# x^T at another place in its tile for the second attention and the second feed-forward

## The chip, the core and the metric

The program runs on one core of a Trainium2 chip. A core has a matrix engine (PE in the profile, with its weight loads as PEld), three engines for elementwise work (DVE, ACT, POOL), a queue engine (SP) that issues the transfers here, and an on-chip memory of 128 partitions. An address below is always a byte offset inside a partition, the same in all 128. The metric is the device time of one execution in microseconds.

## The reference

A decoder trunk of two layers on 256 tokens of width 1024. Each layer is a norm, an attention, a norm and a feed-forward with 2816 hidden columns; the residual stream goes through all of them.

```python
for i in range(DEPTH):
    j = i // N_MIXERS
    if i % N_MIXERS == 0:
        h = h + dilated_mixer(rmsnorm(h, a_norm[j]), a_w_in[j], a_w_out[j])
    else:
        h = h + forgetting_mixer(rmsnorm(h, b_norm[j]), b_w_in[j], b_f[j], b_w_out[j])
    h = h + swiglu(rmsnorm(h, ffn_norm[i]), ffn_w_gu[i], ffn_w_down[i])
return rmsnorm(h, final_norm)
```

All is float32. The kernel splits each operand of a large product into a high and a low part and sums three products (high·high, high·low, low·high), which `mm3` issues one after the other.

## The kernel before

The four stages run one after the other: first attention (up to about 268 us in the profiled execution), first feed-forward (to about 452), second attention (to about 569) and second feed-forward. All weights are streamed from memory through the SP queue, split by ACT (`wh`) and DVE (`wl`), and multiplied.

Each of the four stages starts from the normalized residual stream, transposed, which is called x^T (`xt`). `norm_t` (L160) scales the rows, transposes them on PE into PSUM, and splits them into the tile `xt` with ACT and DVE. The tile has one buffer, which the four stages use in turn. In a partition it is 8 k-tiles of 2 parts (high, low) of 256 float32: 16,384 bytes, every part 1,024 bytes long. The first x^T is allocated at the start of the program. Those of the two feed-forwards come from `out_proj` (L614), which is called for `a_out` and `b_out`, and that of the second attention from the first `mid` (L758).

A matmul has a stationary operand, which a weight load brings in (128 columns of 4 bytes, that is 512 bytes of each partition), and a moving one, which is streamed (256 columns are 1,024 bytes). Three helpers use x^T:

- `proj_feat` (L221): the weights are stationary, x^T is moving, 256 columns. The query and key projections, and all hidden columns of the feed-forwards from the fourth tile on (`up`). A call with both column halves is 2 · 8 · 3 = 48 matmuls.
- `proj_tok` (L201): x^T is stationary, the weights move, 256 columns. Two value projections of the second attention, and the first three tiles of each feed-forward (the "head").
- `proj_pair` (L211): as `proj_tok`, 512 columns (the last products are cut into two of 256). The first two value projections of the second attention.

Beside these, `gates_1` (L782) streams 512 columns of x^T against the small tile `wf` (8 matmuls), and the down projection (`down`, L688) has the activations `ah` and `al` stationary and the weights moving; no x^T is in it.

Where the tiles lie. Tiles get addresses in the order of the pools and tags. The tiles in front of x^T in its pool are multiples of 512 bytes long, as are all tiles of the weight pool, so they all have the address of the weights modulo 512. Behind them stands an unused tile `gap` of 112 float32, 448 bytes; then comes x^T. Modulo 512 x^T therefore begins 64 bytes in front of the weights, and as every slice of it and every slice of the weights starts at a multiple of 512 bytes of its tile, this holds for each pair of operands of these matmuls. Behind x^T the small tiles add up to 64 bytes, and the tiles of the activations (`p`, which holds `ah` and `al`) are at the place of the weights again, at a distance of 0. So are `kr` and `qzh`, `qzl` of the first attention (tag `h`), and `wf`, whose k-tiles step by 256 bytes.

The lines of the gap and of the x^T tile:

```python
    ap.tile([P, 112], F32, tag="gap", name="gap", bufs=1)
    xt = xt_tile()
```

Of the kernel before, what the change touches and what calls it, by code (L numbers as in the profile page):

```python
# [10 lines left out]
F32 = mybir.dt.float32  # L11
F32R = mybir.dt.float32r
# [4 lines left out]
P = 128  # L17
D = 1024
S = 256
KT = D // P  # L20
# [11 lines left out]
def trunk(ctx: ExitStack, tc: tile.TileContext, T, out):  # L32
# [4 lines left out]
    ap = ctx.enter_context(tc.tile_pool(name="ap", bufs=1))  # L37
# [8 lines left out]
    def psum(tag):  # L46
        return ps.tile([P, 512], F32, tag=tag, name=f"ps_{tag}", bufs=2)
# [4 lines left out]
    def load_grow(i):  # L52
        g = ap.tile([P, D], F32, tag="grow", name="grow", bufs=1)
        src = T["norms"]
        nc.sync.dma_start(g, bass.AP(tensor=src.tensor, offset=src.offset + i * D, ap=[[0, P], [1, D]]))
        return g

    def const(name, shape):
        c = cst.tile(shape, F32, name=name)
        nc.sync.dma_start(c, T[name])  # L60
        return c
# [32 lines left out]
    def fm_tile(tag, n, bufs):  # L94
        return tuple(ap.tile([P, n, S], F32R, tag=f"{tag}{x}", name=f"{tag}{x}", bufs=bufs) for x in "hl")
# [1 line left out]
    class XT(tuple):  # L97
        pass

    def xt_tile():  # L100
        full = ap.tile([P, KT, 2, S], F32R, tag="xt", name="xt", bufs=1)
        x = XT((full[:, :, 0, :], full[:, :, 1, :]))
        x.full = full
        return x
# [24 lines left out]
    def weights(nm, i, after=None):  # L129

        upto = order.index((nm, i)) + AHEAD
        while state["next"] <= min(upto, len(order) - 1):
            key = order[state["next"]]
            cuts = []
            ready[key] = piece(key, cuts)
            for cut in cuts:
                cut(after)
            state["next"] += 1
        return ready.pop((nm, i))
# [20 lines left out]
    def norm_t(h, parts, grow, xt, t):  # L160
        with first():
            r = rstd(parts)
            xn = ap.tile([P, D], F32, tag="xn", name="xn", bufs=2)
            for half in range(2):
                c = slice(half * 512, (half + 1) * 512)
                nc.vector.scalar_tensor_tensor(xn[:, c], h[:, c], r, grow[:, c], op0=ALU.mult, op1=ALU.mult)
        for half in range(2):
            tr = psum("tr")
            for k in range(4):
                kk = half * 4 + k  # L170
                nc.tensor.transpose(tr[:, k * P:(k + 1) * P], xn[:, kk * P:(kk + 1) * P], ident)  # L171
            split(xt, lambda x: x[:, half * 4:half * 4 + 4, t * P:(t + 1) * P],
                  tr.rearrange("p (k c) -> p k c", k=4))

    def mm3(o, stat, mov, start, stop, narrow=False):

        (sh, sl), (mh, ml) = stat, mov
        nc.tensor.matmul(o, sh, mh, start=start, stop=False)  # L178
        n = o.shape[-1]
        for s, m, end in ((sh, ml, False), (sl, mh, stop)):  # L180
            for c in range(0, n, n // 2 if narrow else n):
                u = slice(c, c + (n // 2 if narrow else n))
                last = nc.tensor.matmul(o[:, u], s, m[:, u], start=False, stop=end and u.stop == n)  # L183
        return last

    def both(pair, *idx):
        return tuple(x[idx] for x in pair)
# [116 lines left out]
    for i, c in enumerate(room):  # L304
        b = 1 + (i > 1)
        n = S + 512
# [12 lines left out]
        for j in range(b):  # L319
            xk.append(both_k[:, j, :S])  # L320
            wk.append(both_k[:, j, S:])

    ap.tile([P, 112], F32, tag="gap", name="gap", bufs=1)
    xt = xt_tile()

    r_a = []
    lead = [psum("sc") for _ in range(2)]
# [73 lines left out]
    x = []  # L401

    ot = fm_tile("ot", KT, 1)
# [200 lines left out]
    def residual(acc, h, name):  # L604
        hn = hrow(name)
        parts = []
        with first():
            for n in range(2):
                s = slice(n * 512, (n + 1) * 512)
                nc.vector.tensor_tensor(hn[:, s], acc[n], h[:, s], op=ALU.add)  # L610
                parts.append(sq(hn[:, s]))
        return hn, parts

    def out_proj(nm, ot, h, grow, done, banks):  # L614

        ws = [weights(nm, i) for i in range(4)]
        xt = xt_tile()
        res = []

        def part(t, acc, nk):  # L620
            last = None
            for n, k in nk:
                c = (k % 2) * D + n * 512
                last = mm3(acc[n], both(ot, ALL, k, slice(t * P, (t + 1) * P)),
                           both(ws[k // 2], ALL, slice(c, c + 512)), k == 0, k == KT - 1)
            return last

        def cols(ks):
            return [(n, k) for n in range(2) for k in ks]

        for t in range(2):
            acc = [psum(banks[t]) for _ in range(2)]
            if t == 0:

                nk = cols(range(done))
                last = part(t, acc, nk[:done])
                nk = nk[done:]
                for i in sorted(due):
                    with tc.issue_after(last.ins):
                        for fn, a in due[i]:  # L640
                            fn(*a)
                    last = part(t, acc, nk[:2]) or last
                    nk = nk[2:]
                due.clear()
                part(t, acc, nk)
                last = part(t, acc, cols(range(done, KT)))
            else:
                part(t, acc, cols(range(2)))
                with tc.issue_after(last.ins):
                    part(t, acc, cols(range(2, 6)))  # L650
                    norm_t(*res[0], grow, xt, 0)
                    part(t, acc, cols(range(6, KT)))
            res.append(residual(acc, h[t], f"h_{nm}{t}"))
        return res, xt


    def ffn(l, hs, xt, grow, mid):
        acc = {}
        acts = {}
# [77 lines left out]
        with tc.issue_after(last.ins):  # L737
            down(NJ - 2, 1)
            if l == 0:
                down(NJ - 1, 1, (0,))  # L740
            else:
                h1 = hs[1][0][:, 512:]
                with first():
                    nc.vector.tensor_tensor(h1, acc[1][1], h1, op=ALU.add)
            mid(res[0])
            down(NJ - 1, 1, (1,) if l == 0 else None)
        res.append(residual(acc[1], hs[1][0], f"hf{l}1") if l == 0 else (acc[1], hs[1][0]))
        return res

    g_f = load_grow(1)  # L750
    hs, xt = out_proj("a_out", ot, x, g_f, 6, ("sc", "mm"))
    maskb = const("maskb", [P, 3 * P])
    sel = const("sel", [80, NH])
    bf = const("bf", [NH, 1])
    wf32 = const("b_f_in", [P, KT * NH])
    nxt = {}

    def mid(h0):  # L758
        nxt["g"] = load_grow(2)
        nxt["xt"] = xt_tile()  # L760
        norm_t(*h0, nxt["g"], nxt["xt"], 0)

    hs = ffn(0, hs, xt, g_f, mid)
    xt, g_b = nxt["xt"], nxt["g"]

# [66 lines left out]
    ot = fm_tile("ot", KT, 1)  # L832
# [62 lines left out]
    for i, (hq, w) in enumerate(b_units):  # L895
# [36 lines left out]
        for fn, a in due.pop(i, ()):  # L932
            fn(*a)
    g_f = load_grow(3)
    hs, xt = out_proj("b_out", ot, [h for h, _ in hs], g_f, 5, ("mm", "sc"))

    def finish(t, h, parts):
        r = rstd(parts)
# [10 lines left out]
    hs = ffn(1, hs, xt, g_f, mid)  # L949
# [4 lines left out]
    for o, (a, b) in zip(acc, ((0, 512), (512, 256), (768, 256))):  # L954
        s = slice(a, a + b)
# [108 lines left out]
```

## Time and profile before

| | us |
|---|---|
| median of two runs | 760.5 (760.35 to 760.64) |
| the profiled execution, its own time | 761.3 |
| its span, first to last instruction | 759.4 |
| granted clock of PE over the span | 0.997 |

The profiled execution took 0.8 us more than the median, and its span is 1.9 us less than its own time. A rate is read below from the starts of matmuls: they are pipelined, so the duration of a row (276 ns for most) is longer than the step from one start to the next, and it is the step that adds up to the time. In the timeline a row has the start in us, the time to the end of the last instruction merged into the row, engine, line, operation, written and read tiles, columns of the stationary operand, form of the moving one, and the count.

### The profile page before, as it was taken

Reading aid. Unit: us, or ns where it says so; the run is one execution under the profiler, and the core shown is the slowest. Engines: PE = TensorE matmul, PEld = TensorE weight load, DVE = VectorE, ACT = ScalarE, POOL = GpSimd, SP = SyncE. Lnnn points to the kernel's source line nnn. Section 1 sums busy time; section 2 is a strip of 40 time slices with the busy share of each in tenths; the row PEclk is TensorE's granted clock in tenths of the full one; section 3 lists DMA queues with packets and bytes.
Section 4 is the critical chain, followed back from the end, with each engine's and each line's share of the span. In section 5 each row is a group of like instructions: output and inputs, shape, how many; then the busy total and the mean of one; then the engine's idle time right before and its main releaser. Section 6 shows DMA issues by size and latency. Waiting matters only on the chain.

```text
span 759.4 us, 14132 instructions
## 1 busy us (share of the span) xinstructions
PE 749.7 (99%) x5810; PEld 695.6 (92%) x5810; DVE 511.1 (67%) x758; ACT 402.7 (53%) x664; POOL 32.4 (4%) x51
## 2 busy tenths in 40 slices
PE   8999999999999999999999999999999999999996
PEld 7999999999998799999999988999889999999995
DVE  6899987986988476555556374888756655556533
ACT  7737539448538455534445354587645434455521
POOL 1110000010010000000000003100000000000000
PEclk9999999999999999999999999999999999999998
DMA  8855553653555367556567444634426665566601
GB/s 329 281 189 192 168 184 105 211 183 104 188 187 177 95 215 243 195 193 195 186 207 239 147 164 142 220 115 142 135 76 228 224 196 193 186 203 202 216 1 55
DMA packets 38352, 135.01 MB, mean 178 GB/s; under 512 B 4368, under 2 KB 5648, under 8 KB 38288
## 3 DMA queue, kind: packets, MB, share of 16 engines
q1 hardware_dynamic: 38144, 134.01, 53.3%
q8 instruction: 45, 0.74, 0.4%
q14 instruction: 19, 0.16, 0.1%
q10 hardware_dynamic: 144, 0.10, 0.0%
HBM read 133.05 MB, written 1.05 MB: 177 GB/s over the span
## 4 chain that ended last, share of the span: by engine, by line
PE 93%; ACT 2%; issue 2%; DMA 1%; DVE 1%; SPq 0%; POOL 0%; POOLq 0%; ACTq 0%; DVEq 0%
PE ps_mm L183 32%; PE ps_mm L178 17%; PE ps_tr L183 9%; PE ps_sc L183 9%; PE ps_o L183 7%; PE ps_tr L178 5%; PE ps_sc L178 4%; PE ps_o L178 3%; PE ps_tr L275 2%; PE ps_o L286 2%; PE ps_sc L844 1%; DMA otl<-in_lead 1%; ACT wh L73 1%; PE ps_tr L171 1%; PE ps_sc L441 1%
## 5 line engine op out<-in xcount | busy, mean ns | idle before, releaser
L73 ACT ACTIVATE wh<-raw 128x1024 fp32r<-128x1024 f32 x236 | 244.0, 1056 | 220.0 <-PE ps_tr L183 67.3
L75 DVE TENSOR_TENSOR wl<-raw,wh 128x1024 fp32r<-128x1024 f32 x236 | 284.6, 1222 | 99.1 <-ACT wh L73 98.7
L178 PE MATMUL ps_mm<-xt,wh 128*128 128x256 f32 x816 | 227.2, 279 | 0.0
L183 PE MATMUL ps_mm<-xt,wl 128*128 128x256 f32 x816 | 225.8, 277 | 0.1
L183 PE MATMUL ps_mm<-xt,wh 128*128 128x256 f32 x816 | 225.7, 277 | 0.0
L178 PEld LDWEIGHTS ps_mm<-xt,wh 128*128 128x128 f32 x816 | 153.3, 188 | 0.6 <-issue 0.3
L183 PEld LDWEIGHTS ps_mm<-xt,wl 128*128 128x128 f32 x816 | 153.3, 188 | 0.5 <-DVE wl L75 0.5
L183 PEld LDWEIGHTS ps_mm<-xt,wh 128*128 128x128 f32 x816 | 153.4, 188 | 0.1
L183 PE MATMUL ps_tr<-xt,wh 128*128 128x256 f32 x304 | 83.8, 276 | 0.0
L183 PE MATMUL ps_tr<-xt,wl 128*128 128x256 f32 x304 | 83.8, 276 | 0.0
L178 PE MATMUL ps_tr<-xt,wh 128*128 128x256 f32 x304 | 83.6, 276 | 0.0
L685 DVE TENSOR_TENSOR sa<-ps_tr,sa 128x256 f32<-128x256 f32 x38 | 16.1, 424 | 73.6 <-PE ps_tr L183 73.6
L183 PEld LDWEIGHTS ps_tr<-xt,wh 128*128 128x128 f32 x304 | 57.1, 188 | 0.0
L183 PEld LDWEIGHTS ps_tr<-xt,wl 128*128 128x128 f32 x304 | 57.1, 188 | 0.0
L178 PEld LDWEIGHTS ps_tr<-xt,wh 128*128 128x128 f32 x304 | 56.9, 188 | 0.0
L178 PE MATMUL ps_mm<-wh,xt 128*128 128x256 f32 (+1 forms) x160 | 53.1, 332 | 0.0
L183 PE MATMUL ps_mm<-wl,xt 128*128 128x256 f32 (+1 forms) x164 | 52.2, 322 | 0.0
L183 PE MATMUL ps_mm<-wh,xt 128*128 128x256 f32 (+1 forms) x164 | 52.1, 321 | 0.0
L183 PEld LDWEIGHTS ps_mm<-wl,xt 128*128 128x128 f32 x164 | 31.1, 190 | 2.6
L183 PEld LDWEIGHTS ps_mm<-wh,xt 128*128 128x128 f32 x164 | 30.8, 190 | 2.8 <-DVE xt L75 0.3
L178 PEld LDWEIGHTS ps_mm<-wh,xt 128*128 128x128 f32 x160 | 30.4, 190 | 3.0
L183 PE MATMUL ps_sc<-wh,al 128*128 128x512 f32 (+1 forms) x82 | 31.4, 387 | 0.0
(237 smaller groups left out, 1170.3 us busy)
## 6 DMA issues: line engine op xcount, KB each, us to landing
raw<-in_gu SPq DMA_DIRECT2D x88, 512.0 KB, 4.7
raw<-in_a_in SPq DMA_DIRECT2D x68, 512.0 KB, 4.3
raw<-in_dn SPq DMA_DIRECT2D x44, 512.0 KB, 4.7
raw<-in_b_in SPq DMA_DIRECT2D x24, 512.0 KB, 4.8
raw<-in_a_out SPq DMA_DIRECT2D x8, 512.0 KB, 5.3
raw<-in_b_out SPq DMA_DIRECT2D x8, 512.0 KB, 3.9
grow<-in_norms SPq DMA_DIRECT2D x4, 512.0 KB, 6.1
x<-in_x SPq DMA_DIRECT2D x2, 512.0 KB, 5.4
```

Of the source, the lines that this page charges most:

```text
L73: a = nc.scalar.activation(view(hi), src, AF.Copy)
L75: return a, nc.vector.tensor_tensor(view(lo), src, view(hi).bitcast(F32), op=ALU.subtract)
L171: nc.tensor.transpose(tr[:, k * P:(k + 1) * P], xn[:, kk * P:(kk + 1) * P], ident)
L178: nc.tensor.matmul(o, sh, mh, start=start, stop=False)
L183: last = nc.tensor.matmul(o[:, u], s, m[:, u], start=False, stop=end and u.stop == n)
L275: nc.tensor.transpose(tr[:, i * P:(i + 1) * P], b, ident)
L286: nc.tensor.matmul(o[h * HD:(h + 1) * HD], v[:, c:c + HD], w(h), start=start, stop=stop)
L441: nc.tensor.matmul(sc[h][a * 64:a * 64 + 64, o:o + 64], q[hr[h], b // 2, c], k[hr[h], b // 2, c], start=True, stop=True)
L685: nc.vector.tensor_tensor(a, u, sg, op=ALU.mult)
L844: last = nc.tensor.matmul(scs[h][:, qb * P:qb * P + (qb + 1) * P], qz[h][rows[h], pr, qb * P:(qb + 1) * P], kz[h][rows[h], pr, :(qb + 1) * ...
```

## The change

x^T's tile becomes 112 float32 longer and the `gap` tile goes, so that all other tiles stay where they were. Inside the longer tile x^T begins at a place that the caller gives: `front` is the number of bytes by which it lies in front of the weights, modulo 512. The first attention and the first feed-forward get 64, as before (element 112 of the tile, the same address). The second attention gets 256 (element 64, 192 bytes earlier than before), the second feed-forward 128 (element 96, 64 bytes earlier than before). No instruction is added or taken away by the text of the change.

```diff
-    def xt_tile():
-        full = ap.tile([P, KT, 2, S], F32R, tag="xt", name="xt", bufs=1)
+    def xt_tile(front):
+        n = KT * 2 * S
+        at = 128 - front // 4
+        tile = ap.tile([P, n + 112], F32R, tag="xt", name="xt", bufs=1)[:, at:at + n]
+        full = tile.rearrange("p (k x s) -> p k x s", k=KT, x=2)
         x = XT((full[:, :, 0, :], full[:, :, 1, :]))
         x.full = full
         return x
...
-    ap.tile([P, 112], F32, tag="gap", name="gap", bufs=1)
-    xt = xt_tile()
+    xt = xt_tile(64)
...
-    def out_proj(nm, ot, h, grow, done, banks):
+    def out_proj(nm, ot, h, grow, done, banks, front):
...
-        xt = xt_tile()
+        xt = xt_tile(front)
...
-    hs, xt = out_proj("a_out", ot, x, g_f, 6, ("sc", "mm"))
+    hs, xt = out_proj("a_out", ot, x, g_f, 6, ("sc", "mm"), 64)
...
-        nxt["xt"] = xt_tile()
+        nxt["xt"] = xt_tile(256)
...
-    hs, xt = out_proj("b_out", ot, [h for h, _ in hs], g_f, 5, ("mm", "sc"))
+    hs, xt = out_proj("b_out", ot, [h for h, _ in hs], g_f, 5, ("mm", "sc"), 128)
```

## The prediction

> **What bounds the kernel now.** I read the page first, then the matmuls with x^T by stage, then the starts of single matmuls.
>
> ```profile
> PE 749.7 (99%) x5810; PEld 695.6 (92%) x5810; DVE 511.1 (67%) x758; ACT 402.7 (53%) x664; POOL 32.4 (4%) x51
> PE 93%; ACT 2%; issue 2%; DMA 1%; DVE 1%; SPq 0%; POOL 0%; POOLq 0%; ACTq 0%; DVEq 0%
> ```
>
> PE is busy for 99% of the span, and 93% of the chain that ended last is PE. So a nanosecond more or less per matmul is a nanosecond of the time, whichever stage it falls in. The next answer counts the matmuls that read x^T in the stages whose x^T moves: three stretches of the second attention, then the head and the rest of the second feed-forward (stretch, its length, busy time of PE on x^T and count, granted clock, which is full, DMA share, GB/s).
>
> ```profile
> 451.90:472.10 20.20, 19.29 (x106) 1.00 0.54 181
> 472.10:498.05 25.95, 23.55 (x194) 1.00 0.48 163
> 498.62:542.00 43.38, 29.51 (x240) 1.00 0.46 147
> 569.28:593.20 23.92, 17.84 (x144) 1.00 0.68 227
> 593.67:738.40 144.73, 104.96 (x912) 1.00 0.54 179
> ```
>
> By the code, the second attention has 384 matmuls with x^T moving (8 query and key units of 48), 100 with x^T stationary and 256 columns, 46 with 512, and the 8 of the gates. That is 538; the three rows add to 540, since two tails reach over an edge. The second feed-forward has 144 in its head and 912 after it.
>
> What does one cost? Starts tell it. First x^T moving, at its present place of 64 bytes in front of the weights: three times in the second attention, once in the second feed-forward.
>
> ```profile
> 472.11 0.28 PE L178 MATMUL ps_mm<-xt,wh 128*128 128x256 f32 x1
> ...
> 483.41 0.38 PE L824 MATMUL ps_tr<-ident,gates 128*16 128x128 f32 x2
> ...
> 495.21 0.28 PE L178 MATMUL ps_mm<-xt,wh 128*128 128x256 f32 x1
> ...
> 498.05 0.82 PE L275 MATMUL ps_tr<-ident,p 128*128 128x128 f32 x6
> ...
> 499.74 0.28 PE L178 MATMUL ps_mm<-xt,wh 128*128 128x256 f32 x1
> ...
> 501.44 0.27 PE L844 MATMUL ps_sc<-z,z 80*128 80x128 f32 x1
> ...
> 596.41 0.28 PE L178 MATMUL ps_tr<-xt,wh 128*128 128x256 f32 x1
> ...
> 604.57 0.39 PE L178 MATMUL ps_sc<-wh,ah 128*128 128x512 f32 x1
> ```
>
> From 472.11 to 483.41 there are two whole units, 96 matmuls in 11.30 us: 117.7 ns each. From 495.21 to 498.05 there are 24 in 2.84 us, 118.3 ns, the last of them a little longer. From 499.74 to 501.44 there are 15 in 1.70 us: 113.3 ns. From 596.41 to 604.57 there are one and a half units, 72 in 8.16 us: 113.3 ns. The same instructions at the same distance therefore run in two rhythms. In the second attention I take the slow one to last from 472.1 to the transposes at 498.05, and the fast one to follow; the 912 of the feed-forward I take to go like these 72. Now the other distances: x^T stationary (the head, 48 matmuls), `kr` with `qz` (distance 0, 12 matmuls), the activations with the weights (distance 0).
>
> ```profile
> 569.28 0.28 PE L178 MATMUL ps_mm<-wh,xt 128*128 128x256 f32 x1
> ...
> 574.93 0.28 PE L178 MATMUL ps_o<-wh,xt 128*128 128x256 f32 x1
> 45.87 0.28 PE L178 MATMUL ps_sc<-kr,qzh 128*128 128x256 f32 x1
> ...
> 47.29 0.29 PE L178 MATMUL ps_mm<-xt,wh 128*128 128x256 f32 x1
> 593.43 0.40 PE L183 MATMUL ps_o<-wh,al 128*128 128x256 f32 x2
> 593.67 0.29 PE L178 MATMUL ps_mm<-xt,wh 128*128 128x256 f32 x1
> ```
>
> x^T stationary: 5.65 us over 48, 117.7 ns. `kr`: 1.42 over 12, 118.3 ns. Activations: 0.24 over 2, 120 ns. And with 512 columns:
>
> ```profile
> 461.52 0.39 PE L178 MATMUL ps_mm<-wh,xt 128*128 128x512 f32 x1
> ...
> 464.27 2.00 PE L786 MATMUL ps_o<-xt,wf 128*48 128x512 f32 x8
> 466.11 0.40 PE L178 MATMUL ps_mm<-wh,xt 128*128 128x512 f32 x1
> 607.30 0.39 PE L178 MATMUL ps_o<-wh,ah 128*128 128x512 f32 x1
> ...
> 609.34 0.39 PE L178 MATMUL ps_o<-wh,ah 128*128 128x512 f32 x1
> ```
>
> x^T stationary: 2.75 us over 12, 229.2 ns. Gates: 1.84 over 8, 230 ns. Activations: 2.04 over 9, 226.7 ns, which is twice 113.3. The steps cluster, then, at a base of 113.3 ns per 256 columns and at 4.4 to 6.7 ns above it. With 256 columns, the base is seen only at a distance of 64 with x^T moving; at 0, and with x^T stationary, the quoted steps lie above it. I read the difference as two reads of PE, weight load and moving operand, meeting at some distances. That is a reading: no row shows the meeting itself.
>
> **The change part by part.** *Work.* The first attention and first feed-forward keep their addresses: 0. No instruction, transfer or queue entry is added or moved, and no tile but x^T changes its address. The writes of x^T go to other addresses:
>
> ```profile
> L73 ACT ACTIVATE xt<-ps_tr x12: 576/592/603, 265.5 to 576.8; 128x512 fp32r<-128x512 f32 x12
> L75 DVE TENSOR_TENSOR xt<-ps_tr,xt x12: 681/684/692, 266.9 to 577.5; 128x512 fp32r<-128x512 f32 x12
> ```
>
> Eight of each twelve are in the moved stages. Their spread of 27 and 11 ns bounds a change at ±0.3 us in sum (8 · 38 ns), and they stand beside matmuls of the stage before or of the head: 0 taken. If that cover went, the 0.3 us would be paid, by the first matmul that waits for DVE's write.
>
> *Second attention, 64 to 256.* The distance turns to exactly half of 512, so it is the same whichever operand is stationary. No row has it for these matmuls. The nearest are 64 in front (base, or 4.4 above it) and, for x^T stationary, 64 behind (4.4 above). Half of the gates' weight loads lie 256 bytes farther, at 320 (`wf` steps by 256), and the gates take 3.3 ns above their base, which speaks for a cost there. Lower bound of the stage: everything goes to the base. The moving part in the slow rhythm is 192 matmuls (the x194 row less its tails), 192 · 4.4 = 0.84 us; 100 · 4.4 = 0.44 us; 54 with 512 columns · 2.5 = 0.14 us: together −1.4 us. Upper bound: the largest step seen, 120 ns, for all 384 moving, 384 · 6.7 − 0.84 = +1.7 us, and +0.2 us for 100 stationary (120 less 117.7): +1.9 us. I take −1.4 us. The row that it is nearest to is the 113.3 at 64, for the matter looks like a collision, worst at 0, and 256 is as far from 0 as a place can be. What is late next is again PE: it has no other engine to wait for in these rows.
>
> *Second feed-forward, 64 to 128.* After the head, 912 matmuls are at the base. Lower bound 0, for no row has less. Upper bound: 912 · 4.4 = +4.0 us for the slow rhythm, 912 · 6.7 = +6.1 us for the step of 120. I take 0: the nearest row is the 113.3 at 64, and 128 lies farther from 0. For the head the distance with x^T stationary becomes 128 behind; bounds −144 · 4.4 = −0.6 us (base) and 144 · 2.3 = +0.3 us (120). The nearest row is 64 behind, 117.7: 0 taken.
>
> *Sum.* −1.4 us. Against the profiled execution, 761.3 − 1.4 = 759.9; it stood 0.8 over the median, so the median becomes 759.1 us. By the lower bounds it is 760.5 − 2.0 = 758.5 us, by all upper ones 760.5 + 1.9 + 6.1 + 0.3 = 768.8 us.
>
> [...]
>
> **The rivals.** *Nothing happens.* The rhythm may be set by what ran before it and not by the place: the 117.7 of the moving matmuls follows directly on x^T stationary at 472.1, and it ends at 498.05 with the transposes. For it: one distance shows both rhythms. Against it: distance 0 stays above the base where 64 doesn't. Both moved stages then keep their steps, 760.5 us, within 0.4. [...]
>
> *The feed-forward falls into the slow rhythm* (the other side). At 128 the 912 matmuls after the head take 117.7 or 120 instead of 113.3. For it: they are at the base at one distance only, which has its slow rhythm too, and the head would lead into it with 117.7. Against it: 128 is farther from 0, and a down projection stands between every few of them. With no gain in the attention this gives 764.5 to 766.6, with the whole one 763.1 to 765.2. It decides against the gain from 1.4 us / 912 = 1.5 ns per matmul on.
>
> *The base is no floor.* Both 113.3 at distance 64 and 226.7 at distance 0 might hold a meeting that a far distance avoids. The nearest shorter step in the trace is that of a transpose, with the same weight load but 128 columns:
>
> ```profile
> 449.63 1.04 PE L171 MATMUL ps_tr<-ident,xn 128*128 128x128 f32 x8
> 450.42 0.48 PE L178 MATMUL ps_o<-wh,ah 128*128 128x512 f32 x1
> ```
>
> 0.79 over 8, 99 ns. Were the 384 + 912 moving matmuls to reach it, 1296 · 14.3 = 18.5 us would go: 742.0 us, the far end. Against it: two distances with exactly 113.3 per 256 columns look like the rate of the stream itself. [...]
>
> **How the numbers follow.** The forecast, the second attention nearer to the base and the feed-forward kept, has 0.45, and its own range is 758.2 to 760.0. Nothing happens: 0.2. The slow feed-forward: 0.28. A lower base: 0.07. The range from 757.8 to 765.4 takes in the first two whole, and more than half of the third, since its four corners are 763.1 to 766.6: together about 0.82. It leaves out the lower base and the upper corners. Two per cent is 15.2 us, about what a measurement of this kernel can tell from no change. Slower by that needs 11.7 ns on each of 1,296 matmuls, and the largest seen is 6.7: 0.02. Faster by that needs most of the way to the transposes' 99 ns: 0.02. Within: 0.96.
>
> **What would show it.** In the changed kernel: the two units after the value projections (96 matmuls, now 11.30 us) at 10.9 us is right, at 11.3 the history sets the rhythm, at 11.5 it is a worse place. The one and a half units between two down projections at 8.16 us is right; 8.5 or more is the slow rival; 7.9 or less a lower base. The head's first 48 at 5.65 us is as forecast. The first two stages must keep their lengths. What would make the prediction wrong is above all the 912: nearly all of the upper range is theirs. And if the stages come out as told but the span doesn't, a wait has moved that this sum has not seen.

## The result, and the profile after

The changed kernel takes 768.7 us (768.08 and 769.34), against 760.5 before: ratio 1.0108, with a 95% interval of 1.0065 to 1.0151. It is slower, by less than 2%. The forecast was 759.1, the range ended at 765.4. One execution of the kernel before and the first of the kernel with x^T 32 and 48 bytes in front (below) had a mean granted clock of 0.56 and took 1256.9 and 1256.4 us; no figure here rests on them.

Page of the changed kernel: span, busy time of PE and PEld, the chain by engine.

```profile
span 767.4 us, 14132 instructions
PE 757.4 (99%) x5810; PEld 703.0 (92%) x5810; DVE 511.3 (67%) x758; ACT 402.4 (52%) x664; POOL 33.8 (4%) x51
...
PE 94%; DMA 2%; ACT 2%; issue 1%; DVE 1%; POOL 0%; SPq 0%; POOLq 0%; ACTq 0%; DVEq 0%
```

The span grew by 8.0 us and PE's busy time by 7.7, with the same number of instructions on each engine: PE does the same work more slowly. The stretches of the two moved stages, x^T's matmuls alone (stretch, length, busy time and count, granted clock, DMA share, GB/s):

```profile
473.06:500.10 27.04, 24.07 (x194) 1.00 0.48 158
500.40:545.50 45.10, 30.77 (x240) 1.00 0.45 141
572.32:596.30 23.98, 18.04 (x144) 1.00 0.67 225
596.88:746.30 149.42, 109.64 (x912) 1.00 0.53 173
```

The counts and the clock are those of before. The 912 of the feed-forward now have 4.7 us more of busy time (109.64 against 104.96). The steps, by starts in the timeline of the changed kernel: an untouched run of the first feed-forward; two units and a later piece of the second attention; the head and one and a half units of the second feed-forward.

```profile
296.29 0.28 PE L183 MATMUL ps_tr<-xt,wh 128*128 128x256 f32 x1
...
304.45 0.39 PE L183 MATMUL ps_sc<-wh,ah 128*128 128x512 f32 x1
...
473.06 0.28 PE L183 MATMUL ps_mm<-xt,wh 128*128 128x256 f32 x1
...
484.58 0.38 PE L827 MATMUL ps_tr<-ident,gates 128*16 128x128 f32 x2
...
500.85 0.28 PE L183 MATMUL ps_mm<-xt,wh 128*128 128x256 f32 x1
...
503.37 0.82 PE L847 MATMUL ps_sc<-z,z 80*128 80x128 f32 x4
...
572.32 0.29 PE L183 MATMUL ps_mm<-wh,xt 128*128 128x256 f32 x1
...
578.09 0.28 PE L183 MATMUL ps_o<-wh,xt 128*128 128x256 f32 x1
...
599.74 0.28 PE L183 MATMUL ps_tr<-xt,wh 128*128 128x256 f32 x1
...
608.27 0.39 PE L183 MATMUL ps_sc<-wh,ah 128*128 128x512 f32 x1
```

| matmuls of 256 columns | before, ns | after, ns |
|---|---|---|
| first feed-forward, x^T moving (not moved) | 113.3 | 72 in 8.16 us: 113.3 |
| second attention, first two units | 117.7 | 96 in 11.52 us: 120.0 |
| second attention, later | 113.3 | 21 in 2.52 us: 120.0 |
| second feed-forward, head, x^T stationary | 117.7 | 48 in 5.77 us: 120.2 |
| second feed-forward, x^T moving | 113.3 | 72 in 8.53 us: 118.5 |

The sum by these steps: 912 · 5.2 = 4.7 us; in the attention 192 · 2.3 + 192 · 6.7 = 1.7 us; 0.2 us for the head, by its busy time (18.04 against 17.84), for only its first part takes 120.2 ns: about 6.7 us of the 8.0. Of the rest, 0.84 us is there already at 296.29, where the run before had 295.45, in a part that the change doesn't touch; the run with the change in the feed-forward alone (below) has 295.38 there. Most of it goes back to a wait of PE for POOL in the first attention, which the run before doesn't have:

```profile
26.44 0.71 PE L540 MATMUL ps_tr<-ident,rs_a 128*128 128x128 f32 x4 [0.51 <-POOL rs_a L401]
```

Another 0.46 us is a longer wait in front of the scores of the second attention (0.70 us at 488.52, against 0.24 at 486.86 before). The run with the change in the attention alone doesn't have it, so it isn't the place of x^T either.

### The profile page after: what moved, and what is told of

It is laid out like the page before. It is cut to its first block, busy times and chain, and to the rows that moved or that the text cites. A ratio compares the mean times of both kernels' runs of the same rounds, so it can differ in the third digit from the quotient of the medians.

```text
span 767.4 us, 14132 instructions
## 1 busy us (share of the span) xinstructions
PE 757.4 (99%) x5810; PEld 703.0 (92%) x5810; DVE 511.3 (67%) x758; ACT 402.4 (52%) x664; POOL 33.8 (4%) x51
## 4 chain that ended last, share of the span: by engine, by line
PE 94%; DMA 2%; ACT 2%; issue 1%; DVE 1%; POOL 0%; SPq 0%; POOLq 0%; ACTq 0%; DVEq 0%
PE ps_mm L188 32%; PE ps_mm L183 17%; PE ps_tr L188 9%; PE ps_sc L188 9%; PE ps_o L188 7%; PE ps_tr L183 5%; PE ps_sc L183 4%; PE ps_o L183 3%; PE ps_tr L280 2%; PE ps_o L291 2%; PE ps_sc L847 1%; DMA otl<-in_lead 1%; DMA raw<-in_a_in 1%; ACT wh L73 1%; PE ps_tr L176 1%
## 5 line engine op out<-in xcount | busy, mean ns | idle before, releaser
L188 PE MATMUL ps_tr<-xt,wh 128*128 128x256 f32 x304 | 84.7, 279 | 0.0
L183 PE MATMUL ps_tr<-xt,wh 128*128 128x256 f32 x304 | 84.4, 279 | 0.0
```

## The experiments

In the diffs `xt_tile(…)` and the last argument of `out_proj` are bytes in front of the weights; the order of the four stages is first attention, first feed-forward, second attention, second feed-forward.

**One part alone, twice.**

```diff
-        nxt["xt"] = xt_tile(256)
+        nxt["xt"] = xt_tile(64)
```

> x^T at 64 in front everywhere but in the second feed-forward, which stays at 128. Theory 'distance' (the distance of the two operands modulo 512 sets the step from one matmul to the next, stage by stage): the second attention is back at the steps of before, the 912 matmuls of the feed-forward stay at 118.6 ns and its head at about 119 to 120, so 912 x 5.2 ns + 144 x 1.4 ns = 4.9 us over before: 765.4 us (764.9 to 766.0). Rival 'history' (the rhythm is handed on from the stage before): with the attention back at 64, most of the feed-forward falls back to 113.3 and the time is within 1 us of before.

```diff
-    hs, xt = out_proj("b_out", ot, [h for h, _ in hs], g_f, 5, ("mm", "sc"), 128)
+    hs, xt = out_proj("b_out", ot, [h for h, _ in hs], g_f, 5, ("mm", "sc"), 64)
```

> x^T at 64 in front everywhere but in the second attention, which stays at 256. Theory 'distance': 384 matmuls with x^T moving at 120.0, 100 stationary at 119.5, 512 columns at 227 to 230: 1.6 us by the steps alone, 2.2 us by the length of the stage in the two traces: 762.1 to 762.9 us; the feed-forward at 113.3. With the run before it the two parts add to the whole change within 0.7 us. Rival 'history': the feed-forward keeps a part of its slow steps, and the time is over 764 us.

The feed-forward alone: 765.7 us against 761.3 before, ratio 1.0058 (1.0042 to 1.0074). Its attention has the 117.8 of before (96 matmuls from 472.03 to 483.34), its feed-forward 72 in 8.54 us, 118.6. The attention alone: 763.2 against 761.3, ratio 1.0025 (1.0014 to 1.0037), with the feed-forward back at 8.16. So each stage pays for its own place, +4.4 and +1.9 us, and the steps of the second feed-forward are not handed on from the attention. Together they are 6.3 us. The 763.2 is a little over the 762.9 expected.

**All addresses moved, no distance.**

```diff
+    cst.tile([P, 48], F32, name="pad")
     mhalf = cst.tile([P, 1], F32, name="mhalf")
```

> The changed kernel, with an unused tile of 192 bytes in front of all tiles: every address rises by 192 bytes, every distance stays. The x^T of the second attention now lies at the very residue of 512 at which the kernel before has it. Theory 'distance': nothing changes against the changed kernel, 767.5 to 769.3 us, steps 120.0 in the attention and 118.6 in the feed-forward. Rival 'own address' (the step depends on where x^T begins, not on where the weights are): the second attention goes to 113.3 or 117.7, 1.5 to 2.2 us less, and the first feed-forward leaves 113.3, up to 6 us more.

767.6 against 761.3, ratio 1.0084 (1.0066 to 1.0102), which overlaps that of the changed kernel; the difference of 6.3 us is that of the two parts together. The first two units of the second attention, in this kernel's timeline:

```profile
474.06 0.28 PE L184 MATMUL ps_mm<-xt,wh 128*128 128x256 f32 x1
...
485.58 0.38 PE L828 MATMUL ps_tr<-ident,gates 128*16 128x128 f32 x2
```

These 96 take 11.52 us, 120.0 ns, as in the changed kernel. The runs of 72 are 8.16 us in the first feed-forward and 8.54 in the second. x^T's own address is not what counts, though in this kernel the attention's x^T lies where the kernel before has it modulo 512; its distance from the weights is.

**Other distances.** Four kernels with other fronts, each run once.

```diff
-    hs, xt = out_proj("a_out", ot, x, g_f, 6, ("sc", "mm"), 64)
+    hs, xt = out_proj("a_out", ot, x, g_f, 6, ("sc", "mm"), 96)
...
-        nxt["xt"] = xt_tile(256)
+        nxt["xt"] = xt_tile(128)
...
-    hs, xt = out_proj("b_out", ot, [h for h, _ in hs], g_f, 5, ("mm", "sc"), 128)
+    hs, xt = out_proj("b_out", ot, [h for h, _ in hs], g_f, 5, ("mm", "sc"), 80)
```

> x^T 96 in front in the first feed-forward, 80 in the second, 128 in the second attention. Theory 'distance': the three stages show three steps of their own; between 64 (113.3) and 128 (118.6) the step rises, so 96 at 114 to 118 ns, 80 at 113 to 117, and the attention at 118 to 119 with x^T moving. If 64 lies at the edge of a flat stretch, 80 is at 113.3 too. Rival 'only multiples of 64 matter': 80 is at 113.3 and 96 at 113.3 or 118.6, nothing between.

> x^T 160 in front in the first feed-forward, 192 in the second, 384 in the second attention. Theory 'narrow gap' (nearly every distance costs, and 64 is one of few places that doesn't): steps of x^T moving between 117 and 120 ns at all three, so 3.4 to 6.1 us over before from each feed-forward and 0.6 to 1.7 from the attention. Rival 'near or far' (80 to 128 are still too near, a wide free stretch lies farther off): 113.3 to 114 at one of the three at least.

> x^T 320 in front in the first feed-forward, 384 in the second, 448 (that is, 64 behind) in the second attention. As the run with 160 and 192: 117 to 120 ns by 'narrow gap', 113.3 to 114 somewhere by 'near or far'. 384 is measured in two stages of these runs; by 'distance' they agree within 0.3 ns. 448 with x^T moving is the mirror image of 64 with x^T stationary; if only the amount of the distance counted, it would be 113.3; if it counts which operand is ahead, it lies above.

> x^T 448 in front in the first feed-forward, at the place of the weights (512, that is 0) in the second feed-forward and in the second attention. By 'distance' the steps at 0 are those of the other operands at 0 in the kernel before, 118.3 to 120 ns: 912 x 5.0 to 6.7 ns = 4.6 to 6.1 us over before in the second feed-forward. 448 agrees with that of the attention of the run before within 0.3 ns.

For places nearer than 64 the tile needs 16 elements more:

```diff
-        tile = ap.tile([P, n + 112], F32R, tag="xt", name="xt", bufs=1)[:, at:at + n]
+        tile = ap.tile([P, n + 128], F32R, tag="xt", name="xt", bufs=1)[:, at:at + n]
...
-        v = ap.tile([P, 4], F32, tag="rs_a", name="rs_a", bufs=1)
+        v = cst.tile([P, 4], F32, name="rs_a")
...
-                rt = ap.tile([P, 2], F32, tag="rt", name="rt", bufs=1)
+                rt = cst.tile([P, 2], F32, name="rt")
```

> As e8_ffn_32_48, whose run had a granted clock of 0.556 throughout and so says nothing of steps. x^T 32 in front in the first feed-forward and the second attention, 48 in the second feed-forward. Theory 'narrow gap': 117 to 120 ns at both. Rival 'edge': 48 at 113.3 to 114, and the feed-forward as before.

The times of these five were 772.8, 772.6, 766.4, 772.3 and 773.7 us, none below before. Each feed-forward shows the step of its distance in the same place, the first run of 72 matmuls between two down projections. Two kernels' runs, with x^T 320 and 384 in front, then 448 and 0:

```profile
295.42 0.28 PE L183 MATMUL ps_tr<-xt,wh 128*128 128x256 f32 x1
...
303.58 0.39 PE L183 MATMUL ps_sc<-wh,ah 128*128 128x512 f32 x1
...
596.92 0.28 PE L183 MATMUL ps_tr<-xt,wh 128*128 128x256 f32 x1
...
605.46 0.39 PE L183 MATMUL ps_sc<-wh,ah 128*128 128x512 f32 x1
```

```profile
295.02 0.28 PE L183 MATMUL ps_tr<-xt,wh 128*128 128x256 f32 x1
...
303.50 0.40 PE L183 MATMUL ps_sc<-wh,ah 128*128 128x512 f32 x1
...
601.59 0.28 PE L183 MATMUL ps_tr<-xt,wh 128*128 128x256 f32 x1
...
610.23 0.40 PE L183 MATMUL ps_sc<-wh,ah 128*128 128x512 f32 x1
```

| x^T in front, bytes | 72 matmuls of a feed-forward, us | step, ns |
|---|---|---|
| 0 | 8.64 | 120.0 |
| 32 | 8.52 | 118.3 |
| 48 | 8.58 | 119.2 |
| 64 | 8.16 | 113.3 |
| 80 | 8.59 | 119.3 |
| 96 | 8.45 | 117.4 |
| 128 | 8.53 | 118.5 |
| 160 | 8.64 | 120.0 |
| 192 | 8.48 | 117.8 |
| 320 | 8.16 | 113.3 |
| 384 | 8.54 | 118.6 |
| 448 | 8.48 | 117.8 |

Lines 64 and 320, 128 and 384, 192 and 448 agree in pairs, and the 120.0 of the attention at 256 is that of 0. The distance counts modulo 256, not 512; as 0 and 128 differ, not 128 either. Of the nine residues tried, 64 alone is at 113.3 in the feed-forwards; 48 and 80, 16 bytes to either side, cost 6 ns, though 113 to 117 was expected for 80. The first two units of the second attentions agree with the table at 0, 32, 128 and 384: 120.0, 118.3, 118.6 and 118.6 ns. At 448 they don't. The kernel with 320, 384 and 448:

```profile
472.09 0.28 PE L183 MATMUL ps_mm<-xt,wh 128*128 128x256 f32 x1
...
482.98 0.38 PE L827 MATMUL ps_tr<-ident,gates 128*16 128x128 f32 x2
```

These 96 take 10.89 us, 113.4 ns, where the feed-forward at 448 has 117.8; most of the later units of this attention are at 117.8 too. So the residue 192, which is 64 bytes the other way, shows the two rhythms that the kernel before shows at 64, and the agreement within 0.3 ns that was expected for 448 fails. The table's 117.8 at 192 and 448 may be the slow one of the two. Below, a free place is one that shows 113.3 at all: 64 and 192. There is no wide free stretch: the place of the kernel before is a narrow one, and 256 and 0 are the same place.

**x^T at 320 everywhere**, the pair of 64, as a test of the period.

```diff
-    xt = xt_tile(64)
+    xt = xt_tile(320)
```

with 320 in the three other places too.

> x^T 320 bytes in front in all four stages, that is 256 more than before; nothing else. Theory 'modulo 256': every stage has the steps of the kernel before, and the time is within 0.7 us of it. Rival 'modulo 512': the stages other than the first feed-forward, which showed 113.5 at 320, may leave their steps; the 912 of the second feed-forward alone then cost 3.4 us or more.

761.3 against 760.8, ratio 1.0002 (0.9993 to 1.0011), both runs of 72 at 8.16 us. One stretch differs: the last 23 matmuls of the value projections, with x^T stationary, go at 113.5 ns (469.79 to 472.40) where the kernel before has 117.8 (469.40 to 472.11). The period of 256 holds.

**The weights moved for the matmuls with x^T stationary.** The idea was that these want the distance the other way round. The run with 448 in the first feed-forward shows the later part of its head at 113.3, where x^T in front by 192 modulo 256 leaves the stationary operand 64 ahead of the moving one, as 64 does for the others:

```profile
275.55 0.28 PE L183 MATMUL ps_mm<-wh,xt 128*128 128x256 f32 x1
...
283.71 0.28 PE L183 MATMUL ps_mm<-wh,xt 128*128 128x256 f32 x1
```

72 in 8.16 us; the first part of that head is at 117.8. So the weights of these matmuls were moved inside their tiles:

```diff
+    def place(key):
+        nm, i = key
+        if nm[:2] == "gu":
+            return 32 if i < 3 else 0
+        if nm == "b_in" and i % 3 == 2:
+            return 48 if i < 6 else 32
+        return 48 if nm == "a_in" and i > 8 and i % 9 in (5, 8) else 0
...
-            wh, wl = (wp.tile([P, 2048], F32R, tag=y, name=y, bufs=4) for y in ("wh", "wl"))
+            at = place(key)
+            wh, wl = (wp.tile([P, 2112], F32R, tag=y, name=y, bufs=4)[:, at:at + 2048] for y in ("wh", "wl"))
```

> x^T 64 in front in all stages. The weight tiles are 256 bytes longer, so that their buffers lie in turn at 0 and 256 modulo 512, and inside the tile the weights of the two feed-forward heads and of two value projections of the second attention begin 128 bytes later, those of the value projections with 512 columns (both attentions, the first attention's but for its first group and its early tokens' ones) 192 bytes later; for the room the two large masks share one tile, and the small tiles of both attentions too. Theory 'distance modulo 256, stationary less moving': the 1824 matmuls of the feed-forwards with x^T moving stay at 113.5 ns although half of the weights are moved by 256; the heads (now stationary 64 ahead of moving, modulo 256) go from 117.8 to 113.5 to 115; the 512-column ones (now 0) from 230 to 227. 0.5 us less per head at most, 0.3 in the attention, 0.5 in the first attention: 1.2 to 2.5 us under before. Rival 'modulo 512': half of the 1824 leave 113.5, 3 us or more over before. Rival 'history': with the attention's value projections at 113.5, the 192 slow matmuls after them go to 113.3 too, 0.8 us more off; by 'distance' alone they may stay.

762.0 against 760.8, ratio 1.0016 (1.0007 to 1.0024): slower, where a gain was expected. The 72 of both feed-forwards stay at 8.16 us although the weight buffers now alternate between 64 and 320, so the period is right once more. The value projections of the second attention with 256 columns did fall, from 117.8 to about 114 ns, but the 96 query and key matmuls behind them still take 11.30 us, 117.7 ns, so the rival 'history' isn't borne out. Two things went against the expectation. 48 matmuls of the first head, 64 ahead now, still take 5.65 us, 117.7 ns; and a run of 144 in the first attention, whose own distance wasn't changed but which now follows 512-column matmuls at another distance, became slow:

```profile
181.31 0.28 PE L192 MATMUL ps_mm<-xt,wh 128*128 128x256 f32 x1
...
198.28 0.38 PE L289 MATMUL ps_tr<-ident,p 128*128 128x128 f32 x2
```

16.97 us over 144, 117.8 ns, where the kernel before goes from 180.12 to 196.45, 113.4. In the last run below, which moves the same weights but those of the first attention, the 144 are back at 113.4. At a free place there are thus two rhythms, and what ran before seems to choose between them. It is not all that chooses. The changed kernel and that with the change in the attention alone have the same program at the same addresses up to the second attention, yet the same query and key matmuls of their first attention run in different rhythms. First the changed kernel, then the attention alone:

```profile
27.11 0.28 PE L188 MATMUL ps_mm<-xt,wh 128*128 128x256 f32 x1
...
46.72 0.28 PE L183 MATMUL ps_sc<-kr,qzh 128*128 128x256 f32 x1
27.19 0.28 PE L188 MATMUL ps_mm<-xt,wh 128*128 128x256 f32 x1
...
47.57 0.28 PE L183 MATMUL ps_sc<-kr,qzh 128*128 128x256 f32 x1
```

173 matmuls take 19.61 us, 113.4 ns, in one and 20.38 us, 117.8 ns, in the other. That is 0.77 us between two executions which no line of the program explains, more than the gain looked for in the next run. The same stretch is at 117.8 in the traces with all addresses moved and with the weights moved, so the loss of the latter can't be put down to its weights alone.

**A restart.** A transpose that nobody reads, to break the run of matmuls between the value projections and the first query projection of the second attention:

```diff
     later(4, gates_2)
+    nc.tensor.transpose(psum("tr")[:, :P], ident, ident)
```

> x^T 64 in front in all stages, and one transpose of a constant on PE, whose result nobody reads, between the last value projection of the second attention and the first query projection; nothing else. Theory 'two rhythms at one distance': at 64 the steps are 117.7 or 113.3 by how the run of matmuls began; after the transpose the 192 slow matmuls go at 113.3, 0.84 us less, for some 0.2 us that the transpose and the restart cost: 0.6 us under before. Rival: the rhythm belongs to something else that happens from 472 to 498 us (traffic of other engines), and the steps stay at 117.7, the time 0 to 0.3 us over before.

761.2 against 761.2, ratio 1.0002 (0.9993 to 1.0010). The units after the transpose stay slow, by this kernel's timeline:

```profile
472.29 0.27 PE L898 MATMUL ps_tr<-ident 128*128 128x128 f32 x1
472.32 0.36 PE L183 MATMUL ps_mm<-xt,wh 128*128 128x256 f32 x1
...
473.82 0.28 PE L183 MATMUL ps_mm<-xt,wh 128*128 128x256 f32 x1
...
483.71 0.38 PE L827 MATMUL ps_tr<-ident,gates 128*16 128x128 f32 x2
```

From 473.82 to 483.71 there are 84 in 9.89 us, 117.7 ns. From the transpose to 473.82 it is 1.53 us with 12 matmuls, 0.12 over 12 · 117.7 ns; the 0.2 expected for the transpose and the restart was an estimate. A restart alone doesn't do it. The rival, something else that goes on from 472 us, isn't excluded by this run; but the kernel with 448 in this place runs the same stretch at 113.4, and the next one at 113.3.

**Both**: the moved weights of the heads and of the second attention, and a transpose in front of each head and of the first query projection.

```diff
+        if nm == "b_in" and i % 3 == 2:
+            return 48 if i < 6 else 32
+        return 0
...
         dn = {}
         head = []
+        nc.tensor.transpose(psum("tr")[:, :P], ident, ident)
```

> As the run before, with a transpose also in front of each feed-forward head, and with the weights of the heads and of the second attention's value projections moved inside their tiles as in the run with moved weights (128 and 192 bytes), those of the first attention not. By 'distance modulo 256' with 'two rhythms': heads at 113.3 to 115 instead of 117.8, 0.4 us less each for 0.2 us of restart, value projections 0.4 us less, query and key projections 0.8 us less; the first attention as before: 1 to 2 us under before. If a restart doesn't help the heads, 0.3 to 1 us under.

760.7 against 761.2, ratio 0.9987 (0.9978 to 0.9996): faster than the kernel before by 0.1%, at or below the lower end of the 1 to 2 us that were expected. In this kernel the later part of the second head is at the fast rhythm, and so are the first query and key units:

```profile
472.78 0.28 PE L192 MATMUL ps_mm<-xt,wh 128*128 128x256 f32 x1
...
483.32 0.38 PE L839 MATMUL ps_tr<-ident,gates 128*16 128x128 f32 x2
...
578.65 0.28 PE L192 MATMUL ps_mm<-wh,xt 128*128 128x256 f32 x1
...
584.09 0.28 PE L192 MATMUL ps_o<-wh,xt 128*128 128x256 f32 x1
```

93 from 472.78 to 483.32 in 10.54 us are 113.3 ns, and 48 of the head in 5.44 us are 113.3. The units from 492.84 on are still at 117.8, as before. In these runs it took both: the moved weights without a transpose in front left the heads at 117.7, and the transpose behind value projections at 117.8 left the query and key units at 117.7. But no run has the transposes of the heads alone, and the first units of the attention with x^T at 448 reached 113.4 with neither. So this is not shown to be a rule, and what in the engine holds the rhythm stays open: no row shows it.

## Why the prediction was wrong

*What bounds the kernel* was right: PE alone, and a nanosecond per matmul is a nanosecond of the time (PE is busy for 99% of the span, and its busy time grew by 7.7 us where the span grew by 8.0). The two moved stages gave +6.3 us in the runs of one part each, by steps within the bounds that the prediction had worked out.

*"I take −1.4 us … 256 is as far from 0 as a place can be"* is the first step that failed. It took the 512 of the change's description for the period. The period is 256 (64 and 320, 128 and 384, 192 and 448 agree), so 256 is 0, and the steps of 0 came: 120.0 ns. The stage alone cost +1.9 us, the upper bound given.

*"I take 0: the nearest row is the 113.3 at 64, and 128 lies farther from 0"* is the second, and the dear one. It assumed that the cost falls with the distance from 0. The runs at 48 and 80 show a free place narrower than 32 bytes, and from 32 to 160 the other places have 117 to 120. 128 costs 5.2 ns on each of 912, 4.7 us. The same holds for the head: 0 taken, 0.2 us measured.

*The rivals.* "The feed-forward falls into the slow rhythm" came nearest. Its 118.5 ns lies between the two corners, but it is what 128 and 384 show in all their feed-forwards and in the first units of the attentions there (118.5 to 118.6), and not the slow rhythm of 117.7. The rival had 0.28, and was paired only with an attention that gains or stays, which is why the range ended too early: all upper bounds together were 768.8. Nothing in the trace tied a far distance to a free place. The gates, which the prediction held against 256, don't bear on it: by the period of 256 both halves of their weight loads lie at 64. "Nothing happens" by history falls as a cause of this result, since each stage alone keeps its cost, though at a free place one distance does show two rhythms. "The base is no floor" finds no support: of twelve places none has a step below 113.3.

## What to carry to other kernels

A step that some placement makes shorter says nothing of its neighbours (113.3 ns at 64 bytes, 119.2 and 119.3 at 48 and 80): between two addresses where the trace has no row, both bounds belong in the range, for all stages at once. Before placing operands of PE, sweep the distance in several stages of one kernel and read it by starts; one run gives several points, and the period shows in pairs. Sweep each place in more than one stage, too: 448 bytes in front gave 117.8 ns in a feed-forward and 113.4 in the first units of an attention. And where one place has two rates, a difference between two traces can come from a stage that nobody touched, as the 0.77 us of the first attention did; read all stages before a small gain or loss is put down to the change.

## What the runs showed of the hardware

For matmuls of 256 columns, the distance between stationary and moving operand acts modulo 256 bytes (64 and 320 at 113.3 ns, 128 and 384 at 118.5 and 118.6). Of nine residues only 64 and 192 were seen at 113.3, and the neighbours of 64, 16 bytes off, cost nearly as much as distance 0 (119.2 and 119.3 against 120.0 ns). This was not expected; nor was it that at these two places the same matmul runs steadily at 113.3 or at 117.7 ns, even with the same program up to there (113.4 and 117.8 in the first attention). A mechanism is not shown: the steps above the base lie between 4.1 and 6.7 ns, and that weight load and moving operand meet was the author's reading, which no row shows.
